# A decoder block on one core: Strassen's seven block products in half of the feed-forward's second product

## The chip, the cores and the metric

One core of one Trainium2 chip runs the whole kernel. The metric is the device time of one execution in microseconds, the median of several runs.

## The reference

A decoder block for 256 tokens of width 2048: gated short convolution and sparse attention side by side, a layer norm, then a feed-forward of width 8192, a gated per-layer embedding and a second layer norm. The change lies in the last part:

```python
x = _layer_norm(DN_ALPHA * x + mixed @ w_mix_out[i], ln1_g[i], ln1_b[i])

h = jnp.square(jax.nn.relu(x @ w_mlp_up[i])) @ w_mlp_down[i]
ple = (p[i] @ w_ple[i]) * jax.nn.sigmoid(x @ w_ple_gate[i])
x = _layer_norm(DN_ALPHA * x + h + ple, ln2_g[i], ln2_b[i])
```

`x` is 256 x 2048, `w_mlp_up` 2048 x 8192 and `w_mlp_down` 8192 x 2048, all float32.

## The kernel before

**Precision.** Each float32 operand is split in two float32r parts, a high part (ACT copies it, rounding) and a low part (DVE subtracts the high part from the original). A product is three matmuls: high x high, low x high, high x low.

**Weights.** `wchunk` (line 83) loads 512 KB of a weight matrix by SP's queue into `raw` (four buffers), and makes `whi` on ACT (line 91, four buffers) and `wlo` on DVE (line 93, three buffers). Each of the 648 chunks of the kernel goes this way.

**Two forms of product.** `wstat` (line 96) keeps weights stationary: a block of 256 columns of weights against all 256 tokens, 16 k-tiles in four chunks. For each k-tile it issues two matmuls of 512 columns (line 110: high weights against both parts of the tokens) and two of 256 (line 117: low weights against the high tokens). `xstat` (line 127) keeps tokens stationary: a block of 512 weight columns moves past them, 16 k-tiles in eight chunks, and for each k-tile six matmuls of 512 (lines 139, 140, 143), three for each 128 tokens.

**The feed-forward** (line 750 on) has four chunks of 2048 hidden columns. In each, the up stage is eight `wstat` blocks ("pairs" below, since each gives two tiles of 128 hidden columns). After each, `ev_up` adds the two parts in PSUM, applies relu and square, and splits the result into `h`. Then the down stage is four `xstat` blocks over `h` (`down`, line 775), added into `y`. In the fourth chunk the last block has its weights loaded ahead (`last_weights`, line 791).

**Order.** The program is written in sequence; a scheduling layer then orders the instructions of each engine and sets the semaphores. `issue_after` holds an instruction behind a named one. Each engine and each DMA queue takes its instructions in that order.

**Other names.** The gate stage (lines 714 to 728) multiplies `ple` by a sigmoid, and loads `gb` (g and b of the first layer norm, broadcast) through POOL's queue. `residual` (line 687) forms g, b and the residual sum in `y`, one 512-column piece after each of the first eight up blocks. PSUM has eight banks: four for `mm`, two `sc`, one `tp`, one `po`.

Of the kernel before, what the change touches and what calls it, by code (L numbers as in the profile page):

```python
# [10 lines left out]
F32 = mybir.dt.float32  # L11
F32R = mybir.dt.float32r
# [33 lines left out]
def block_kernel(ctx: ExitStack, tc: tile.TileContext, x, p, w_in, conv_w, cmp_pe_k, cmp_w1_k, cmp_w2_k,  # L46
# [12 lines left out]
    ps_mm = ctx.enter_context(tc.tile_pool(name="ps_mm", bufs=4, space=bass.MemoryType.PSUM))  # L59
    ps_sc = ctx.enter_context(tc.tile_pool(name="ps_sc", bufs=2, space=bass.MemoryType.PSUM))  # L60
    ps_tp = ctx.enter_context(tc.tile_pool(name="ps_tp", bufs=1, space=bass.MemoryType.PSUM))
    ps_po = ctx.enter_context(tc.tile_pool(name="ps_po", bufs=1, space=bass.MemoryType.PSUM))
# [14 lines left out]
    def load_raw(src, nk, n):  # L77

        raw = wp.tile([P, nk, n], F32, tag="raw", name="raw", bufs=4)
        nc.sync.dma_start(raw, src.rearrange("(k p) n -> p k n", p=P))  # L80
        return raw

    def wchunk(src, nk, n, behind=None):


        raw = load_raw(src, nk, n)
# [9 lines left out]
    def wstat(src, c0, mov, evac, r0=0, nk=4, ahead=None, behind=None):  # L96


        ps = [ps_mm.tile([P, 2, T], F32, tag="mm", name="mm") for _ in range(2)]
        for k0 in range(0, KT, nk):  # L100
            hi, lo = wchunk(src[r0 + k0 * P:r0 + (k0 + nk) * P, c0:c0 + 256], nk, 256,
                            behind(k0 // nk) if behind is not None else None)
            for kk in range(nk):
                kt = k0 + kk
                if ahead is not None:
                    ahead(kt)

                def high():
                    for f in range(2):
                        last_mm[0] = nc.tensor.matmul(  # L110
                            ps[f].rearrange("p a t -> p (a t)"), hi[:, kk, f * P:(f + 1) * P],
                            mov[:, kt].rearrange("p a t -> p (a t)"), start=(kt == 0), stop=(kt == KT - 1),
                            skip_group_check=True).ins

                def low():
                    for f in range(2):
                        last_mm[0] = nc.tensor.matmul(ps[f][:, 1, :], lo[:, kk, f * P:(f + 1) * P],  # L117
                                                      mov[:, kt, 0, :], start=False, stop=False,
                                                      skip_group_check=True).ins
# [4 lines left out]
        for f in range(2):  # L124
            evac(f, ps[f][:, 0, :], ps[f][:, 1, :])

    def xstat(src, c0, n, sta, evac, r0=0, nkt=KT, ahead=None, behind=None):

        ps = [ps_mm.tile([P, n], F32, tag="mm", name="mm") for _ in range(NT)]
        for k2 in range(nkt // 2):  # L130
            hi, lo = wchunk(src[r0 + k2 * 256:r0 + (k2 + 1) * 256, c0:c0 + n], 2, n,
# [100 lines left out]
    with tc.tile_pool(name="front", bufs=1) as fp:  # L232
# [79 lines left out]
        def compress(i, w1, w2):  # L312
# [3 lines left out]
            for l4 in range(CMP_LEN // 4):  # L316
                hi, lo = wchunk(w1[0][l4 * 512:(l4 + 1) * 512, :], 4, HID)
# [357 lines left out]
    x1_lo, gated = [], []  # L675
# [11 lines left out]
    def residual(t, j):  # L687

        cs = slice(j * 512, (j + 1) * 512)
        v = y[:, t, cs]  # L690
        nc.vector.tensor_mul(v, v, gb[:, 0, cs])
        nc.vector.tensor_add(v, v, gb[:, 1, cs])
        nc.vector.scalar_tensor_tensor(v, v, ALPHA, ple[:, t, cs], op0=ALU.mult, op1=ALU.add)
# [20 lines left out]
    for j in range(4):  # L714
        cs = slice(j * 512, (j + 1) * 512)

        def ev_gate(t, ps):
            sg = post.tile([P, 512], F32, tag="sg", name="sg")
            nc.scalar.activation(sg, ps, AF.Sigmoid)
            gated.append(nc.vector.tensor_mul(ple[:, t, cs], sg, ple[:, t, cs]).ins)  # L720

        run(xstat(w_ple_gate, j * 512, 512, x1, ev_gate, ahead=x1_ahead if j == 0 else None,
                  behind=(lambda k2: x1_lo[k2 - 1] if k2 else normed) if j == 0 else None))
        if j in (1, 3):

            with after(gated[2 * j - 1]):
                nc.vector.memset(gb[:, j // 2, 0:1], 0.0)
            nc.gpsimd.dma_start(gb[:, j // 2, :], (ln1_g, ln1_b)[j // 2].to_broadcast([P, D]))


    stats2 = post.tile([P, NT, 4, 6], F32, tag="st", name="stats2", bufs=1)
    gb2 = big.tile([P, 2, D], F32, tag="O", name="gb2")
# [17 lines left out]
    done_up = []  # L750
    for c in range(4):
        if c % 2 == 0:
            h = big.tile([P, KT, 2, T], F32R, tag="B", name="h")
        else:
            h = post.tile([P, KT, 2, T], F32R, tag="C", name="h", bufs=1)
        for f2 in range(0, KT, 2):

            def ev_up(f, a, b):
                m = post.tile([P, T], F32, tag="m", name="m", bufs=3)
                nc.scalar.activation(m, a, AF.Copy)  # L760
                nc.vector.tensor_add(m, m, b)
                nc.vector.scalar_tensor_tensor(m, m, 0.0, m, op0=ALU.max, op1=ALU.mult)
# [102 lines left out]
```

## Time and profile before

| | us |
|---|---|
| median of 3 runs (1834.59 to 1834.60) | 1834.59 |
| the profiled execution | 1835.34 |
| its span, first to last instruction | 1833.3 |
| PE busy | 1818.7 |
| DVE busy | 1132.0 |
| ACT busy | 867.7 |
| one up stage (eight `wstat` blocks) | 89.32 |
| one down stage (four `xstat` blocks) | 87.05 |

PE is TensorE's matmuls, DVE VectorE, ACT ScalarE, POOL GpSimd, SP the engine that issues most DMAs. A matmul's record ends by a model, so the pace of a stream of matmuls is read from start to start: the length of a stage over the number of its matmuls.

### The profile page before, as it was taken

The numbers are of one execution on the slowest core, as the hardware profiler recorded it, in microseconds if no ns is written. First come the engines' busy times: TensorE is split into PE (matmuls) and PEld (weight loads), VectorE is DVE, ScalarE is ACT, GpSimd is POOL, SyncE is SP. The second block draws the span as 40 slices with busy tenths as digits, with TensorE's granted clock in tenths as the row PEclk, the third lists the DMA queues.
The fourth block names the chain that finished last, engine by engine and source line by source line (L and its number), as shares of the span: only waits on it lengthen the run. The fifth ranks groups of instructions, "written<-read, shape, count | busy, mean of one in ns | idle before, by whom it ended". The sixth has DMA issues, their size and how long they took to land.

```text
span 1833.3 us, 24899 instructions
## 1 busy us (share of the span) xinstructions
PE 1818.7 (99%) x9412; PEld 1552.1 (85%) x9412; DVE 1132.0 (62%) x1657; ACT 867.7 (47%) x1207; POOL 24.7 (1%) x37
## 2 busy tenths in 40 slices
PE   9999999999999999999999999999999999999997
PEld 7889888888888888888888888888888888888886
DVE  6776777777787444455555656765665556556664
ACT  5555555455555444444443744543444345434550
POOL 1000000000000000000000000000000000000001
PEclk9999999999999999999999999999999999999999
DMA  8777665555656666666655567655665666566671
GB/s 249 229 244 213 176 174 171 172 164 170 173 162 198 221 195 193 191 191 188 192 185 195 176 221 234 190 191 194 193 187 194 191 208 217 189 195 190 196 246 46
DMA packets 261272, 352.92 MB, mean 193 GB/s; under 512 B 11125, under 2 KB 175317, under 8 KB 260384
## 3 DMA queue, kind: packets, MB, share of 16 engines
q1 hardware_dynamic: 256384, 338.08, 60.1%
q0 software_dynamic: 2112, 8.81, 1.5%
q10 hardware_dynamic: 2656, 4.46, 0.7%
q8 instruction: 73, 1.20, 0.3%
q14 instruction: 47, 0.39, 0.1%
HBM read 349.17 MB, written 2.12 MB: 192 GB/s over the span
## 4 chain that ended last, share of the span: by engine, by line
PE 60%; issue 37%; DMA 1%; DVE 0%; POOL 0%; ACT 0%; POOLq 0%; SPq 0%
PE mm L110 16%; PE mm L143 10%; PE mm L140 10%; PE mm L139 10%; PE mm L117 8%; PE mm L807 1%; DMA rawl<-in_w_mlp_down_dram 1%; PE pss L471 1%; PE ph L321 1%; PE tp L194 1%; PE po L543 1%; PE tp L534 1%; PE po L550 0%; DMA xnat<-in_x_dram 0%; ACT wh L71 0%
## 5 line engine op out<-in xcount | busy, mean ns | idle before, releaser
L93 DVE TENSOR_TENSOR wlo<-raw,whi 128x1024 fp32r<-128x1024 f32 (+2 forms) x648 | 780.1, 1205 | 595.7 <-PE mm L143 337.9
L91 ACT ACTIVATE whi<-raw 128x1024 fp32r<-128x1024 f32 (+2 forms) x648 | 677.4, 1047 | 728.0 <-PE mm L140 444.1
L110 PE MATMUL mm<-xT,whi 128*128 128x512 f32 x1280 | 405.5, 399 | 0.1
L110 PE MATMUL mm<-x,whi 128*128 128x512 f32 x1024 | 316.8, 395 | 0.0
L117 PEld LDWEIGHTS mm<-xT,wlo 128*128 128x128 f32 x1280 | 233.8, 189 | 50.9 <-DVE wlo L93 0.2
L117 PE MATMUL mm<-xT,wlo 128*128 128x256 f32 x1280 | 249.0, 280 | 0.0
L117 PEld LDWEIGHTS mm<-x,wlo 128*128 128x128 f32 x1024 | 187.9, 188 | 42.5
L110 PEld LDWEIGHTS mm<-xT,whi 128*128 128x128 f32 x1280 | 199.4, 190 | 3.7 <-ACT whi L91 1.2
L117 PE MATMUL mm<-x,wlo 128*128 128x256 f32 x1024 | 196.7, 279 | 0.0
L140 PE MATMUL mm<-whi,h 128*128 128x512 f32 x480 | 186.7, 389 | 0.0
L139 PE MATMUL mm<-whi,h 128*128 128x512 f32 x480 | 186.7, 389 | 0.0
L110 PEld LDWEIGHTS mm<-x,whi 128*128 128x128 f32 x1024 | 158.4, 189 | 2.8
L143 PE MATMUL mm<-wlo,h 128*128 128x512 f32 x480 | 147.9, 389 | 0.4 <-DVE wlo L93 0.4
L139 PE MATMUL mm<-whi,xT 128*128 128x512 f32 (+1 forms) x352 | 130.1, 373 | 0.0
L140 PE MATMUL mm<-whi,xT 128*128 128x512 f32 (+1 forms) x352 | 130.0, 373 | 0.0
L143 PEld LDWEIGHTS mm<-wlo,h 128*128 128x128 f32 x480 | 90.0, 188 | 19.4 <-DVE wlo L93 0.8
L140 PEld LDWEIGHTS mm<-whi,h 128*128 128x128 f32 x480 | 90.1, 188 | 18.8
L139 PEld LDWEIGHTS mm<-whi,h 128*128 128x128 f32 x480 | 90.1, 188 | 18.7
L143 PE MATMUL mm<-wlo,xT 128*128 128x512 f32 (+1 forms) x352 | 102.7, 373 | 0.0
L139 PEld LDWEIGHTS mm<-whi,xT 128*128 128x128 f32 x352 | 66.1, 188 | 11.2
L140 PEld LDWEIGHTS mm<-whi,xT 128*128 128x128 f32 x352 | 66.1, 188 | 11.2
L143 PEld LDWEIGHTS mm<-wlo,xT 128*128 128x128 f32 x352 | 63.4, 188 | 10.5
(226 smaller groups left out, 1776.3 us busy)
## 6 DMA issues: line engine op xcount, KB each, us to landing
raw<-in_w_in_dram SPq DMA_DIRECT2D x228, 512.0 KB, 3.7
raw<-in_w_mlp_up_dram SPq DMA_DIRECT2D x128, 512.0 KB, 3.9
raw<-in_w_mlp_down_dram SPq DMA_DIRECT2D x120, 512.0 KB, 4.0
raw<-in_w_conv_out_dram SPq DMA_DIRECT2D x32, 512.0 KB, 3.7
raw<-in_w_attn_out_dram SPq DMA_DIRECT2D x32, 512.0 KB, 3.6
raw<-in_w_mix_out_dram SPq DMA_DIRECT2D x32, 512.0 KB, 3.7
raw<-in_w_ple_gate_dram SPq DMA_DIRECT2D x32, 512.0 KB, 3.9
raw<-in_w_in_dram SPq DMA_DIRECT2D x16, 280.0 KB, 3.2
```

The lines of the kernel that those rows point to most:

```text
L91: nc.scalar.activation(hi, raw, AF.Copy)
L93: last_wlo[0] = nc.vector.tensor_sub(lo, raw, f32(hi)).ins
L110: last_mm[0] = nc.tensor.matmul(ps[f].rearrange("p a t -> p (a t)"), hi[:, kk, f * P:(f + 1) * P], mov[:, kt].rearrange("p a t -> p (a t)" ...
L117: last_mm[0] = nc.tensor.matmul(ps[f][:, 1, :], lo[:, kk, f * P:(f + 1) * P], mov[:, kt, 0, :], start=False, stop=False, skip_group_check= ...
L139: nc.tensor.matmul(ps[t], sta[:, kt, 0, ts], hi[:, kk, :], start=(kt == 0), stop=False)
L140: nc.tensor.matmul(ps[t], sta[:, kt, 1, ts], hi[:, kk, :], start=False, stop=False)
L143: last_mm[0] = nc.tensor.matmul(ps[t], sta[:, kt, 0, ts], lo[:, kk, :], start=False, stop=(kt == nkt - 1)).ins
L194: nc.tensor.transpose(tp[:, k, t * P:(t + 1) * P], nat[:, t, (kt + k) * P:(kt + k + 1) * P], ident)
L321: nc.tensor.matmul(ph, blk[:, i, l].rearrange("p a n -> p (a n)"), part[:, k, :], start=(part is hi and l == 0), stop=(part is lo and l == ...
L471: nc.tensor.matmul(ps, q[:, g, a, t * P:(t + 1) * P], kT[:, j, c, c0:c0 + n], start=(i == 0), stop=(i == 2))
L534: nc.tensor.transpose(tp[:, b, k, :], s[:, b, 1 - k if t and b == 0 else k], ident)
L543: nc.tensor.matmul(po, vn[:, b, 0, a, vs], pT[:, c, b, 0:2], start=(n == 0 and b == 0), stop=False, skip_group_check=True)
```

## The change

**Seven products.** In chunks 0 to 2, `down` computes only the columns 1024 to 2047 as before. For columns 0 to 1023, each pair p of k-tiles is a product of 2 x 2 blocks: the tokens in two halves of 128, the hidden columns in two tiles of 128, the weight columns in two halves of 512. Seven block products (Strassen's, in the form with few sums) take the place of eight. Six are accumulated over p in six PSUM banks (`products`, 18 matmuls for each p). The seventh, plain one comes last, as 24 matmuls from weights that are loaded a second time.

**What feeds them.** `up` makes four sums of blocks of h on DVE (`sa`) and splits them (`sums`). `load` fetches the 1 MB of weights of a pair as one transfer; `b_forms` splits the two plain blocks, `t_sums` makes four sums of blocks on DVE, and `t_forms` splits those. After the last product ten DVE operations and one ACT copy combine the six banks into `y`.

**Where.** `products(p - 2)` and the preparation of pair p - 1 are written between the chunks of pair p; the scheduling layer moves them further.

**`ev_up`** becomes: ACT copies both PSUM banks, DVE adds, ACT applies Relu and Square, then the split, 512 columns at a time.

**Order in `wstat`, everywhere in the kernel.** All 512-column matmuls of a chunk come together, then its 256-column ones, and in every other chunk (and the last) the other way round. In the feed-forward (`ps` given) the matmuls of one PSUM bank also come together.

**The rest.** `residual` is taken apart by operation and woven into the gate stage, with the loads of `gb` ahead of it. PSUM is divided anew before the feed-forward. `h` has one buffer in place of two; `wl` and the later `gb2` move. Nothing else changes.

```diff
-            for kk in range(nk):
-                kt = k0 + kk
...
-                for part in ((high, low) if kt < KT - 1 else (low, high)):
-                    part()
+            last = k0 + nk == KT
+            parts_ = (low, high) if last or ahead is None and k0 // nk % 2 == 1 else (high, low)
+            if apart:
+                order = [(part, kk, f) for part in parts_ for f in range(2) for kk in range(nk)]
+                if last:
+                    order.sort(key=lambda o: o[2])
+            else:
+                order = [(part, kk, f) for part in parts_ for kk in range(nk) for f in range(2)]
+            for part, kk, f in order:
+                part(kk, f)
             yield
...
+    def up(c, p, banks):
+
+        ps = [b.rearrange("p (a t) -> p a t", a=2) for b in banks]
+        yield from wstat(w_mlp_up, c * 2048 + p * 256, x1, None, ps=ps)
+        ab = post.tile([P, 2, 2, T], F32, tag="m2", name="ab", bufs=2)
+        for f in range(2):
+            nc.scalar.activation(ab[:, f], ps[f], AF.Copy)
+        m = ab[:, :, 0, :]
+        nc.vector.tensor_add(m, m, ab[:, :, 1, :])
+        nc.scalar.activation(m, m, AF.Relu)
+        nc.scalar.activation(m, m, AF.Square)
+        split(m, h[:, 2 * p:2 * p + 2, 0, :], h[:, 2 * p:2 * p + 2, 1, :])
         if c < 3:
-            run(*(down(j)[0] for j in range(4)))
+
+            sa = post.tile([P, 4, P], F32, tag="pn", name="sa", bufs=1)
+            b11, b12, b21, b22 = (m[:, k, t * P:(t + 1) * P] for t in range(2) for k in range(2))
+            nc.vector.tensor_add(sa[:, 0, :], b21, b22)
+            nc.vector.tensor_sub(sa[:, 1, :], sa[:, 0, :], b11)
+            nc.vector.tensor_sub(sa[:, 2, :], b11, b21)
+            nc.vector.tensor_sub(sa[:, 3, :], b12, sa[:, 1, :])
+            sums[p] = post.tile([P, 4, 2, P], F32R, tag="sg", name="sums")
+            split(sa, sums[p][:, :, 0, :], sums[p][:, :, 1, :])
...
+        def load(p):
+            if p % 2 == 0:
+                raws[p] = post.tile([P, 2, 1024], F32, tag="rs", name="rs", bufs=1)
+            else:
+                raws[p] = tr[:, 4:8].rearrange("p (k a) n -> p k (a n)", k=2)
+            nc.sync.dma_start(raws[p], rows[:, p, :, 0:1024])
+
+        def b_forms(p):
+            r = raws[p]
+            b = forms[:, 8 + p % 2 * 4:12 + p % 2 * 4]
+            split(back(r, 0, (1536, 2), (1, 512)), b[:, 0:2], b[:, 2:4])
+
+        def t_sums(p):
+            r = raws[p]
+            nc.vector.tensor_sub(tf[:, 0:2], r[:, :, 512:], r[:, 0, :].rearrange("p (a n) -> p a n", a=2))
+            nc.vector.tensor_sub(tf[:, 2], r[:, 1, 512:], tf[:, 0])
+            nc.vector.tensor_sub(tf[:, 3], tf[:, 2], r[:, 1, :512])
+
+        def t_forms(p):
+            for i in (0, 2):
+                split(tf[:, i:i + 2], forms[:, i:i + 2], forms[:, 4 + i:6 + i])
+
+        def products(p, which):
...
+                for i, (a, w) in enumerate(((0, hi), (1, hi), (0, lo))):
+                    last_mm[0] = nc.tensor.matmul(acc[n], first[:, a, :], forms[:, w, :], start=(p == 0 and i == 0),
+                                                  stop=(p == 7 and i == 2)).ins
+
+        prep = (b_forms, t_sums, t_forms)
+        for p in range(8):
+            pair = up(c, p, [bank(6), bank(7)] if p == 1 else [bank(0), bank(1)])
+            for i in range(4):
+                if p >= 2 and i in (0, 2):
+                    products(p - 2, (5, 7, 6, 4) if i else (1, 3))
+                next(pair)
+                if i == 2:
+                    load(p)
+                if p >= 1 and i < 3:
+                    prep[i](p - 1)
+            run(pair)
+        products(6, (1, 3, 5, 7, 6, 4))
+        third = down(c, 2, [bank(0), bank(1)])[0]
+        for i in range(8):
+            next(third)
...
+        run(down(c, 3, [bank(2), bank(3)])[0])
+        ps = bank(4)
+        for q in range(0, 8, 2):
+            hi, lo = wchunk(rows[:, q:q + 2, 1, 0:512], 2, 512)
...
```

**The order on PE, third pair of the second chunk.** Before, in every up block, with `mm` the PSUM banks, `x_9126` the tokens:

```order
L117 MATMUL mm<-x_9126,wlo 128x256 x2
L110 MATMUL mm<-x_9126,whi 128x512 x2
L117 MATMUL mm<-x_9126,wlo 128x256 x2
L110 MATMUL mm<-x_9126,whi 128x512 x2
L117 MATMUL mm<-x_9126,wlo 128x256 x2
```

In the changed kernel, from the end of that pair through the fourth (`u` and `s` are PSUM banks, L860 the block products; those of the second pair stand here):

```order
L116 MATMUL u<-x_9126,wlo 128x256 x4
L110 MATMUL u<-x_9126,whi 128x512 x4
L860 MATMUL s<-forms,h 128x512 x3
L860 MATMUL s<-forms,sums 128x512 x12
L860 MATMUL s<-forms,h 128x512
L110 MATMUL u<-x_9126,whi 128x512 x4
L116 MATMUL u<-x_9126,wlo 128x256 x2
L110 MATMUL u<-x_9126,whi 128x512 x4
L116 MATMUL u<-x_9126,wlo 128x256 x14
L110 MATMUL u<-x_9126,whi 128x512 x8
L860 MATMUL s<-forms,h 128x512 x2
L110 MATMUL u<-x_9126,whi 128x512 x8
```

The sizes, which took turns by two, stand in runs, and 16 of the 18 block products have moved to the front of the pair.

**The order on DVE at the same place.** Before, one up block:

```order
L93 TENSOR_TENSOR wlo<-raw,whi 128x1024 x3
L761 TENSOR_TENSOR m<-m,mm 128x256 x2
L762 SCALAR_TENSOR_TENSOR m<-m 128x256 x2
L72 TENSOR_TENSOR h<-m,h 128x256
L93 TENSOR_TENSOR wlo<-raw,whi 128x1024
L72 TENSOR_TENSOR h<-m,h 128x256
```

In the changed kernel, from the add that ends the third pair (L792) to just before the next one; the first `wlo` here is that of the fourth pair's last chunk:

```order
L792 TENSOR_TENSOR ab<-ab 128x2x256
L73 TENSOR_TENSOR forms<-tr,forms 128x1024 x2
L800 TENSOR_TENSOR sa<-ab 128x128
L802 TENSOR_TENSOR sa<-ab 128x128
L843 TENSOR_TENSOR tr<-tr 128x1024
L801 TENSOR_TENSOR sa<-sa,ab 128x128
L73 TENSOR_TENSOR h<-ab,h 128x2x256
L92 TENSOR_TENSOR wlo<-raw,whi 128x1024
L803 TENSOR_TENSOR sa<-ab,sa 128x128
L92 TENSOR_TENSOR wlo<-raw,whi 128x1024
L73 TENSOR_TENSOR sums<-sa,sums 128x4x128
L73 TENSOR_TENSOR forms<-tr,forms 128x1024
```

Two low parts of forms and the sums now stand between the add and the low part of the next weight chunk.

**The order on SP at the end of the second chunk.** Before, the down stage and the next up stage are two rows:

```order
L80 DMA raw<-in_w_mlp_down_dram 128x2x512 x32
L80 DMA raw<-in_w_mlp_up_dram 128x4x256 x32
```

In the changed kernel (`rs` and `tr` receive the 1 MB loads, line 834; the last four `raw` of the down weights are the seventh product's):

```order
L834 DMA rs<-in_w_mlp_down_dram 128x2x1024
L85 DMA raw<-in_w_mlp_down_dram 128x2x512 x9
L834 DMA tr<-in_w_mlp_down_dram 128x2x1024
L85 DMA raw<-in_w_mlp_down_dram 128x2x512 x4
L834 DMA rs<-in_w_mlp_down_dram 128x2x1024
L85 DMA raw<-in_w_mlp_down_dram 128x2x512 x4
L834 DMA tr<-in_w_mlp_down_dram 128x2x1024
L85 DMA raw<-in_w_mlp_up_dram 128x4x256 x19
```

The next chunk's first four 1 MB loads have moved among the loads of this chunk's last blocks.

## Rows read from the trace of the kernel before

**Rows 1.** The page, part 1: busy us (share of the span) xinstructions

```profile
PE 1818.7 (99%) x9412; PEld 1552.1 (85%) x9412; DVE 1132.0 (62%) x1657; ACT 867.7 (47%) x1207; POOL 24.7 (1%) x37
```

**Rows 2.** Waits of PE, whole span: us in total, times, longest us

```profile
PE pw L258 <- DVE tab L272: 1.5, 1, 1.5
PE tp L194 <- DMA xnat<-in_x_dram: 1.0, 2, 0.5
PE mm L143 <- DVE wlo L93: 0.4, 1, 0.4
```

**Rows 3.** Stages: down, up, down, up (chunks 0 to 2)

```profile
core 0: us, PE busy (x) PEld busy (x) DVE busy (x) ACT busy (x) POOL busy (x), PEclk, DMA share, GB/s
1204.73:1291.78 87.05, 87.05 (x385) 72.10 (x384) 46.50 (x48) 35.49 (x37) 0.00 (x0) 1.00 0.60 193
1291.78:1381.10 89.32, 89.32 (x513) 77.98 (x512) 55.17 (x77) 42.78 (x61) 0.00 (x0) 1.00 0.64 189
1381.10:1468.15 87.05, 87.05 (x385) 72.07 (x384) 44.69 (x45) 35.49 (x37) 0.00 (x0) 1.00 0.60 193
```

**Rows 4.** Waits in the up stage 1291.78 to 1381.10

```profile
ACT whi L91 <- PE mm L110: 27.8, 16, 1.9
DVE wlo L93 <- PE mm L117: 21.8, 16, 1.6
```

**Rows 5.** PE in order of time, a run of 256s; start us, us recorded

```profile
61.43 0.63 PE L321 MATMUL ph<-whi,blk 128*120 128x256 f32 x4
61.90 0.63 PE L321 MATMUL ph<-wlo,blk 128*120 128x256 f32 x4
62.36 0.62 PE L110 MATMUL mm<-xT,whi 128*128 128x512 f32 x2
```

**Rows 6.** PE in order of time, where one up block meets the next

```profile
1301.99 0.64 PE L117 MATMUL mm<-x,wlo 128*128 128x256 f32 x4
1302.46 1.09 PE L110 MATMUL mm<-x,whi 128*128 128x512 f32 x4
1303.39 0.40 PE L117 MATMUL mm<-x,wlo 128*128 128x256 f32 x2
```

**Rows 7.** Groups of instructions by form: xcount | busy us, mean ns

```profile
L93 DVE TENSOR_TENSOR wlo<-raw,whi 128x1024 fp32r<-128x1024 f32 x223 | 272.8, 1224 | 225.4 <-PE mm L143 111.2 <-PE mm L117 70.5 <-issue 38.9
L72 DVE TENSOR_TENSOR x<-m,x 128x512 fp32r<-128x512 f32 x8 | 5.5, 689 | 4.4 <-ACT x L71 4.3
L343 DVE TENSOR_TENSOR g<-g,g 128x120 f32<-128x120 f32 x2 | 0.6, 283 | 0.1
L71 ACT ACTIVATE wh<-rawl 128x1024 fp32r<-128x1024 f32 x8 | 8.5, 1062 | 11.4 <-DMA rawl<-in_w_mlp_down_dram 11.4
L602 ACT ACTIVATE sg<-mm 128x512 f32<-128x512 f32 x16 | 8.6, 585 | 4.2 <-PE mm L143 4.2
L71 ACT ACTIVATE x<-m 128x512 fp32r<-128x512 f32 x8 | 5.0, 630 | 0.1
L745 ACT ACTIVATE y<-y,nm,r 128x512 f32<-128x512 f32 x2 | 1.6, 816 | 34.8 <-DVE nm L737 34.8
```

**Rows 8.** DVE in order of time, dependent operations and one that is not

```profile
1198.04 0.69 DVE L691 TENSOR_TENSOR y<-y,ple_gb 128x512 f32<-128x512 f32 x1
1198.76 0.69 DVE L692 TENSOR_TENSOR y<-y,ple_gb 128x512 f32<-128x512 f32 x1
1199.40 1.23 DVE L93 TENSOR_TENSOR wlo<-raw,whi 128x1024 fp32r<-128x1024 f32 x1
1200.55 0.69 DVE L693 SCALAR_TENSOR_TENSOR y<-y,ple_gb 128x512 f32<-128x512 f32 x1
```

**Rows 9.** The ten microseconds with the most traffic

```profile
590.00:600.00 10.00, 10.00 (x46) 8.29 (x45) 3.81 (x4) 5.33 (x6) 0.00 (x0) 1.00 0.99 382
```

**Rows 10.** The last two of the four gate blocks

```profile
1071.90:1115.42 43.52, 43.52 (x194) 36.04 (x192) 22.02 (x21) 18.94 (x21) 0.54 (x1) 1.00 0.67 218
```

More of the change, by code (lines that the diff above doesn't have):

```diff
@@ L102, in wstat @@
                             behind(k0 // nk) if behind is not None else None)
-            for kk in range(nk):
-                kt = k0 + kk
[L105 to L119, printed above, removed]
-                for part in ((high, low) if kt < KT - 1 else (low, high)):
-                    part()
+            if ahead is not None:
+                for kk in range(nk):
+                    ahead(k0 + kk)
@@ L123, in wstat, with xstat @@
             yield
-        for f in range(2):
+        for f in range(2 if evac is not None else 0):
             evac(f, ps[f][:, 0, :], ps[f][:, 1, :])
-    def xstat(src, c0, n, sta, evac, r0=0, nkt=KT, ahead=None, behind=None):
-        ps = [ps_mm.tile([P, n], F32, tag="mm", name="mm") for _ in range(NT)]
+    def xstat(src, c0, n, sta, evac, r0=0, nkt=KT, ahead=None, behind=None, ps=None):
+        if ps is None:
+            ps = [ps_mm.tile([P, n], F32, tag="mm", name="mm") for _ in range(NT)]
@@ L685, in x1_turn, with residual, gb_load, steps_of @@
         x1_lo.append(split(m, x1[:, kt0:kt0 + 2, 0, :], x1[:, kt0:kt0 + 2, 1, :]))
-    def residual(t, j):
+    def residual(i, j):
         cs = slice(j * 512, (j + 1) * 512)
[L690 to L693, printed above, removed]
+        for t in range(NT):
+            v = y[:, t, cs]
+            with after(last_wlo[0]):
+                if i == 2:
+                    nc.vector.scalar_tensor_tensor(v, v, ALPHA, ple[:, t, cs], op0=ALU.mult, op1=ALU.add)
+                else:
+                    nc.vector.tensor_tensor(v, v, gb[:, i, cs], op=(ALU.mult, ALU.add)[i])
+    def gb_load(dst, i, v):
+        with after(last_wlo[0]):
+            nc.vector.memset(dst[:, i, 0:1], 0.0)
+        nc.gpsimd.dma_start(dst[:, i, :], v.to_broadcast([P, D]))
+    def steps_of(*calls):
+        for f, *args in calls:
+            f(*args)
+            yield
     normed = x1_norm(0)
@@ L719, in ev_gate, with bank @@
             nc.scalar.activation(sg, ps, AF.Sigmoid)
[L720 to L728, printed above, removed]
+            nc.vector.tensor_mul(ple[:, t, cs], sg, ple[:, t, cs])
+        places, side = (((), ()),
+                        ((0, 4), ((gb_load, gb, 0, ln1_g), (gb_load, gb, 1, ln1_b))),
+                        ((1, 2, 3, 4, 5, 6), [(residual, 0, i) for i in range(4)] + [(residual, 1, 0), (residual, 1, 1)]),
+                        ((1, 2, 3, 4, 6), ((residual, 1, 2), (residual, 1, 3), (residual, 2, 0), (residual, 2, 1),
+                                           (residual, 2, 2))))[j]
+        weave(xstat(w_ple_gate, j * 512, 512, x1, ev_gate, ahead=x1_ahead if j == 0 else None,
+                    behind=(lambda k2: x1_lo[k2 - 1] if k2 else normed) if j == 0 else None),
+              places, steps_of(*side))
+    residual(2, 3)
+    psum.close()
+    ps_s = ctx.enter_context(tc.tile_pool(name="ps_s", bufs=1, space=bass.MemoryType.PSUM))
+    ps_u = ctx.enter_context(tc.tile_pool(name="ps_u", bufs=2, space=bass.MemoryType.PSUM))
     stats2 = post.tile([P, NT, 4, 6], F32, tag="st", name="stats2", bufs=1)
-    gb2 = big.tile([P, 2, D], F32, tag="O", name="gb2")
+    def bank(i):
+        if i < 2:
+            return ps_u.tile([P, 512], F32, tag="u", name="u")
+        return ps_s.tile([P, 512], F32, tag=f"s{i - 2}", name="s")
     def finish(t, mine=1536):
```

134 lines of the change are left out of this document (84 added, 50 removed).

## The prediction, made before the changed kernel ran

> **What bounds the kernel now.** First the page's busy shares: PE has work for 99% of the span, DVE for 62%, ACT for 47% [rows 1]. A busy PE alone says little, so second comes the list of what PE waited for: three entries, 2.9 us in 1833, one of them, 0.4 us, for a low part from DVE [rows 2]. Third, the stages of the feed-forward: an "up" stage takes 89.32 us and a "down" stage 87.05 us, PE fills both, and in an up stage DVE works 55 us and ACT 43 us of 89 [rows 3]. In that stage ACT and DVE wait for PE, 16 times each, 1.7 and 1.4 us a time, and not the other way [rows 4]. So the span is PE's matmul stream; a change is worth the matmul time that it removes, as long as DVE, ACT and the weight transfers still come before PE.
>
> **The rates.** A down stage is 384 matmuls of 512 columns (4 column blocks x 16 k-tiles x 6): 87.05/384 = 226.7 ns each. An up stage is 8 blocks of 32 matmuls of 512 columns and 32 of 256. At 226.7 ns the 512s are 58.04 us of the 89.32, which leaves 31.28/256 = 122.2 ns for a 256 in the present order, two 512s and two 256s in turn. The granted clock is 1.00 in these stages (its upper level, 2.4 GHz).
>
> **Part 1, fewer matmuls.** In three chunks the half of the down product with columns 0 to 1023 had 192 matmuls of 512. Seven block products instead of eight make 168: 144 woven into the up stage and 24 behind the last column block. 3 x 24 = 72 matmuls go, 72 x 226.7 ns = **16.3 us**. All of this is on PE, so all of it is on the path.
>
> **Part 2, the order inside a column block.** Everywhere that weights are the stationary side, PE now takes the 512s of a chunk together and then its 256s, and every other chunk the other way round. In the built order the size changes 394 times in place of 2084 over the 72 blocks (2304 matmuls of each size). What a longer run is worth is not in the trace as such. Best case: eight 256s in a row took 0.93 us, 116.3 ns each [rows 5], with the 512s at 226.7; then 5.9 ns per pair of sizes, for the 81% of changes that go: 2304 x 5.9 x 0.81 = 11.0 us. Worst case: where one block meets the next there are four 256s in 0.47 us and four 512s in 0.93 us, 350.0 ns for the two against 348.9 in turn [rows 6]: a loss of 2304 x 1.1 ns = 2.5 us. The new runs are 8 to 16 long, nearer to the down stage and to the run of eight than to runs of four; I take a gain of **6 us**.
> What the Trainium skill says bears on both parts: its page "TensorE: Matmul & The Clock Gate", section "Back-to-back issue gap", gives N/2.4 + 2.5 ns for a matmul at full clock, 215.8 ns for 512 columns and 109.2 for 256, with no word of a mix. By that rule part 1 is 72 x 215.8 = 15.5 us and part 2 nothing. The rows above are slower by 11 and 13 ns, so the rule misses something that order may change, and the rows decide.
>
> **Part 3, what DVE and ACT get.** From row durations [rows 7], for one of the eight column-block pairs of an up stage with its products: DVE has 4 low parts x 1.22, the add and the low part of h 2 x 0.69, four sums of 128 columns x 0.29 (nearest row: 120 columns at 0.28), their low part 0.69, one low part of the plain weight blocks 1.22, the weight sums 1.22 + 2 x 0.69, and two low parts of these 2 x 1.22: 14.4 us. PE has 11.17 + 18 x 0.2267 = 15.25 us. ACT has 4 x 1.06 + 2 x 0.585 + 4 x 0.63 + 3 x 1.06 = 11.1 us (Relu and Square, not in the trace, are taken as the copy of 512, 0.63; Identity with scale at 0.82 would add 0.4). So DVE is at 94% by plain sums. DVE operations that don't need each other overlap: the one at 1200.55 starts 0.08 before the end of the one at 1199.40, while a dependent one at 1198.76 starts 0.03 after its source [rows 8]. Between the two DVE's pair costs 13.1 to 14.9 us. Work fits, without room to spare.
> Against this stands the Trainium skill, page "VectorE: DVE Perf Modes", section "The DRAIN you can't avoid": the next operation does not start until the pipe has emptied. By that rule the lower of the two DVE figures falls away and DVE stands at 94% or more; the row at 1200.55 speaks for overlap where nothing is shared.
> Whether it also comes in time is a matter of order. In the order shown for the third pair, from PE's end of a pair (t = 0): PE does 16 products (3.63), two weight chunks (5.58), 2 products (0.45), a third chunk (2.79), and at 12.45 needs the low part of the fourth chunk. DVE must first have the PSUM copies (about 0.8), the add (to 1.5), and two low parts of forms, whose buffers come free after 6 and after 12 products (1.36, 2.72), each behind ACT's copy (1.06): the second is done at 2.72 + 1.06 + 1.22 = 5.0. Then two sums 0.57, a weight sum 1.22, a sum 0.29, the low part of h 0.69 and the low part that PE needs 1.22: **9.0 against 12.45**, 3.4 us ahead. The PSUM banks that the next pair writes are free after about 0.8 and 1.5, and PE wants them at 3.63. So I cost this part at nothing; if the 3.4 us go, every microsecond behind them counts 18 times (six pairs in three chunks).
>
> **Part 4, the seams.** Near the end of a chunk DVE has ten combining operations of 512 (10 x 0.69 = 6.9 us) among the low parts of the third column block, then PE runs through four weight transfers in 24 matmuls, 5.4 us, less time per transfer than anywhere before. The lower bound is nothing; the upper is all ten in front of a low part that PE needs, 6.9 us x 3. DVE's buffers of three low parts and the eight chunks of the fourth column block absorb most of it. I take **2 us** for the three seams, with 10 us for the range.
>
> **Part 5, transfers.** A chunk moved 64 loads of 0.52 MB, 33.6 MB; now 2.1 MB are read again for the seventh product, 35.7 MB in about 171 us (89.32 + 360 x 0.2267), 209 GB/s against 193 and 189 now [rows 3]. In the seam it is more: three loads of 1 MB and twelve of 0.5 MB in about 28 us, 330 GB/s. The trace has 382 GB/s over 10 us with the queues 99% busy [rows 9]. It fits, and its shortfall is in the seam's range above. On SP's queue the big loads stand among the weight loads; each waits for a DVE step that the next weight load nearly waits for too.
>
> **Part 6, the rest.** The 24 residual operations (0.69 each, 16.6 us of DVE) leave the first up stage for the last two gate blocks, where DVE works 22 us of 43.5 [rows 10]; the two broadcast loads of g and b on POOL's queue, each behind a DVE memset of one column, both start in the second gate block now, and nothing but these operations waits for them: nothing for PE. The end (last matmul to last store) has the same operations: nothing.
>
> **The sum.** The profiled execution took 1835.34 us, 2.0 over its span of 1833.3, and 0.75 more than the median of the runs, 1834.59. 1835.34 - 16.3 - 6 + 2 = 1815.0, and 0.75 less for the runs: **1814.3 us**. Ends: 16.3 + 11.0 and no seam loss give 1807.3; 16.3, a loss of 2.5 in the order and 10 at the seams give 1830.8, an unlikely pair, so I stop at 1827.
>
> **Rivals.**
> A, the order is worth nothing: the 512s stay at 232 ns in a stage that has 256s too, in any order. For it: the run of four [rows 6]. Against: the steady 226.7 of the down stage. 1814.3 + 6 = 1820.3 us. (The Trainium skill's section named in part 2 would have it so.)
> B, slower: DVE and ACT in lockstep with PE. Each form is written only after the products that read its buffer, first by ACT and then by DVE, and all low parts stand behind it in DVE's one queue. If DVE can't use its waits, a pair costs 14.4 of work, 0.8 for the copies and 2.4 (1.36 + 1.06) until the first form: 17.6 against 15.25, 2.4 us x 18 = 42 us, so 1856 us. It turns slower than before when each of the 18 pairs loses more than (22.3 - 2)/18 = 1.1 us. Against: the 3.4 us of lead, and that the waits lie beside one another.
> C, the seams cost their upper bound, 20.7 us in place of 2: 1833.0, no change that can be told.
>
> **Chances.** Forecast 0.65, A 0.22, B 0.07, C 0.06. A measurement here tells 0.2% (3.7 us) from no change. Faster 0.87, same 0.06, slower 0.07. Eight in ten are held by 1806 to 1827: forecast, A, and the lower part of the seam costs.
>
> **What would show it.** PE's count falls by 72. Part 1: block products at 227 ns each. Part 2: a block of 64 in the early stages (before the feed-forward) takes 11.08 us instead of 11.17; at 11.17 A is right, and under 11.05 the best case. Part 3: PE's list of waits stays at a few us; B shows as waits of PE for the low part of a fourth chunk or for a form, every pair. Part 4: waits of PE just behind the combining operations or at the four late transfers. The forecast is wrong above all if PE's waits for DVE in the three up stages add up to more than 10 us.

## The result, and the profile of the changed kernel

The changed kernel takes 1817.95 us, the median of five runs (1817.47 to 1820.43), against 1834.59: the ratio is 0.9912, 95% interval 0.9901 to 0.9923. That is 16.6 us less, where 20.3 were forecast. The profiled execution took 1817.73 us with a span of 1815.9; the prediction's own sum for it was 1815.0.

The page's first part, to be laid beside [rows 1] (busy us, share of the span, instructions):

```profile
PE 1801.0 (99%) x9340; PEld 1544.0 (85%) x9340; DVE 1236.2 (68%) x1778; ACT 959.9 (53%) x1302; POOL 24.7 (1%) x37
```

PE has 72 matmuls less and is still busy for 99% of the span. DVE has 104 us more work and ACT 92 us, and PE hardly waits longer for them than before. The list of PE's waits over the whole span (us in total, times, longest), which answers to [rows 2]:

```profile
PE pw L267 <- DVE tab L281: 1.5, 1, 1.5
PE tp L203 <- DMA xnat<-in_x_dram: 0.7, 1, 0.7
PE mm L116 <- DVE wlo L92: 0.6, 1, 0.6
PE mm L148 <- ACT whi L90: 0.3, 1, 0.3
PE u L110 <- ACT whi L90: 0.2, 1, 0.2
```

Only the last of them lies in the three chunks with block products. The 0.6 us (at 22 us) and the 0.3 us (at 114) lie in the early stages and come with the new order: all nine traces of kernels with that order have both, and the two with the old order, here and below, have 0.1 us at the first place and nothing at the second. So the kernel is bound as before, by PE's stream, and the question is what this stream costs now. Two stretches, the whole second chunk (up, products and what is left of the down stage) and the up stage of the fourth, where no products are; they answer to [rows 3]:

```profile
core 0: us, PE busy (x) PEld busy (x) DVE busy (x) ACT busy (x) POOL busy (x), PEclk, DMA share, GB/s
1287.95:1458.89 170.94, 170.94 (x874) 146.06 (x872) 138.79 (x171) 105.13 (x126) 0.00 (x0) 1.00 0.64 209
1629.79:1717.27 87.48, 87.48 (x505) 77.14 (x504) 48.98 (x51) 53.22 (x69) 1.09 (x2) 1.00 0.69 222
```

The second chunk took 89.32 + 87.05 = 176.37 us and takes 170.94: 5.43 less, and 24 matmuls of 226.7 ns are 5.44. The products and the new order together gave what was forecast for the products alone; the kernel with the old order, below, tells the two apart. The second line has 504 of the 512 matmuls of its up stage, since 8 of 512 columns were drawn ahead into the end of the third chunk; with 8 x 0.2267 it is 89.29 us, against 89.32. The new order gave next to nothing there. PE in order of time at the start of that stage (start us, us recorded; a run's real length is the distance to the next start):

```profile
1629.79 2.08 PE L116 MATMUL u<-x,wlo 128*128 128x256 f32 x16
1631.70 3.82 PE L110 MATMUL u<-x,whi 128*128 128x512 f32 x16
1635.36 1.11 PE L116 MATMUL u<-x,wlo 128*128 128x256 f32 x8
1636.31 0.40 PE L110 MATMUL s<-x,whi 128*128 128x512 f32 x1
1636.54 0.65 PE L116 MATMUL u<-x,wlo 128*128 128x256 f32 x4
1637.02 1.09 PE L110 MATMUL u<-x,whi 128*128 128x512 f32 x4
1637.95 0.64 PE L116 MATMUL u<-x,wlo 128*128 128x256 f32 x4
1638.42 1.09 PE L110 MATMUL u<-x,whi 128*128 128x512 f32 x4
```

Sixteen 256s take 1.91 us (119 ns each), sixteen 512s 3.66 (228.8 ns). A run of four 512s takes 0.93 (232.5 ns), as in [rows 6]. The runs are there; what they save is small, and at a block's end runs of four are left.

### The profile page after: what moved, and what is told of

Its sections match the earlier page's. It is cut to its first block, busy times and chain, and to the rows that moved or that the text cites. A ratio compares the mean times of both kernels' runs of the same rounds, so it can differ in the third digit from the quotient of the medians.

```text
span 1815.9 us, 24871 instructions
## 1 busy us (share of the span) xinstructions
PE 1801.0 (99%) x9340; PEld 1544.0 (85%) x9340; DVE 1236.2 (68%) x1778; ACT 959.9 (53%) x1302; POOL 24.7 (1%) x37
## 4 chain that ended last, share of the span: by engine, by line
PE 97%; DMA 1%; DVE 1%; ACT 0%; issue 0%; POOLq 0%; POOL 0%; SPq 0%; ACTq 0%; DVEq 0%
PE mm L110 16%; PE mm L148 10%; PE mm L149 10%; PE mm L152 10%; PE u L110 9%; PE mm L116 8%; PE s L860 5%; PE u L116 5%; PE s L110 4%; PE s L116 2%; PE s L148 2%; PE s L149 2%; PE s L152 2%; PE u L149 2%; PE u L152 2%; PE u L148 2%
## 5 line engine op out<-in xcount | busy, mean ns | idle before, releaser
L110 PE MATMUL mm<-xT,whi 128*128 128x512 f32 x1280 | 313.5, 393 | 0.0
L110 PE MATMUL u<-x,whi 128*128 128x512 f32 x736 | 190.4, 392 | 0.2 <-ACT whi L90 0.2
L116 PE MATMUL mm<-xT,wlo 128*128 128x256 f32 x1280 | 181.6, 285 | 0.6 <-DVE wlo L92 0.6
L116 PEld LDWEIGHTS mm<-xT,wlo 128*128 128x128 f32 x1280 | 170.0, 190 | 8.2 <-DVE wlo L92 0.8
L110 PEld LDWEIGHTS u<-x,whi 128*128 128x128 f32 x736 | 132.4, 188 | 24.1 <-ACT whi L90 0.8
L116 PEld LDWEIGHTS u<-x,wlo 128*128 128x128 f32 x736 | 100.9, 190 | 7.6
L116 PE MATMUL u<-x,wlo 128*128 128x256 f32 x736 | 103.1, 282 | 0.0
L73 DVE TENSOR_TENSOR forms<-tr,forms 128x1024 fp32r<-128x1024 f32 x60 | 72.3, 1220 | 25.0 <-ACT forms L72 24.9
L860 PE MATMUL s<-forms,sums 128*128 128x512 f32 x288 | 73.2, 389 | 0.0
L110 PE MATMUL s<-x,whi 128*128 128x512 f32 x288 | 71.9, 392 | 0.0
L72 ACT ACTIVATE forms<-tr 128x1024 fp32r<-128x1024 f32 x60 | 62.2, 1050 | 10.4 <-PE s L860 6.7
L860 PEld LDWEIGHTS s<-forms,sums 128*128 128x128 f32 x288 | 54.0, 188 | 11.4
```

Of the source, the lines that this page charges most:

```text
L72: last_hi[0] = nc.scalar.activation(hi, src, AF.Copy).ins
L73: last_lo[0] = nc.vector.tensor_sub(lo, src, f32(hi)).ins
L110: last_mm[0] = nc.tensor.matmul(ps[f].rearrange("p a t -> p (a t)"), hi[:, kk, f * P:(f + 1) * P], mov[:, k0 + kk].rearrange("p a t -> p ( ...
L860: last_mm[0] = nc.tensor.matmul(acc[n], first[:, a, :], forms[:, w, :], start=(p == 0 and i == 0), stop=(p == 7 and i == 2)).ins
```

## The experiments

**What a run of one size is worth.** Four kernels are the kernel before with another order in its column blocks and nothing else. With `order` in place of the loop over k-tiles (`high` and `low` are the matmuls of 512 and 256 columns):

```
 r1:  order = [(part, kk, f) for kk in range(nk) for f in range(2) for part in (high, low)]
 r4:  order = [(part, kk, f) for k1 in range(0, nk, 2) for part in (high, low)
               for kk in range(k1, k1 + 2) for f in range(2)]
 r8:  order = [(part, kk, f) for part in (high, low) for kk in range(nk) for f in range(2)]
 r16: the same, with (low, high) in every other chunk
```

In each, the low part comes first at the very end of a block, as in the kernel before. This turn joins two runs, so half of the matmuls of r8 stand in runs of 16, and a quarter of those of r4 in runs of 8.

> The kernel before with the changed order in its column blocks and nothing else: all 512s of a chunk, then its 256s, every other chunk the other way round, so runs of 16. Up stage of the second chunk 89.32 us before. Prediction (a longer run is worth 2.6 ns per pair of sizes): the up stage 88.65 us, the kernel 6 us faster, 1828.6. Theory 1 (each change of size costs 3.0 ns, (89.32 - 256 x 0.3461)/240, whatever the run ahead; 32 changes per stage left): 88.70 us, kernel 1829 to 1830. Theory 2 (what one cycle of sizes costs grows with the run; a cycle of 16 and 16 took 3.654 + 1.913 us in the changed kernel): 16 x 5.567 = 89.07 us, kernel 1832 to 1833. Rival A: 89.32 and 1834.6.

> The kernel before with runs of 8 (all 512s of a chunk, then its 256s, the same way in each chunk; 48 changes of size per up stage in place of 240). Up stage of the second chunk, 89.32 before: theory 1 (fixed price per change) 88.74 us; theory 2 (price per cycle grows with the run) 89.1 to 89.4 us; rival A 89.32.

> The kernel before with runs of 4 (two k-tiles' 512s, then their 256s; 112 changes of size per up stage in place of 240). Up stage of the second chunk, 89.32 before: theory 1 (fixed price per change) 88.93 us; theory 2 (a cycle of 4 and 4 took 0.93 + 0.47 us) 89.4 to 89.6 us, slower than runs of 2; rival A 89.32.

> The kernel before with runs of 1 (a 512 and a 256 in turn; 496 changes of size per up stage in place of 240). Up stage of the second chunk, 89.32 before: theory 1 (fixed price per change) 90.1 us; theory 2 sets no value for it beyond less than 89.4 us if the price of a cycle falls with the run; rival A 89.32.

The up stage of the second chunk, with the columns as above, for runs of 1:

```profile
1293.87:1384.27 90.40, 90.40 (x514) 78.44 (x513) 54.37 (x77) 42.83 (x61) 0.00 (x0) 1.00 0.62 187
```

of 4:

```profile
1293.07:1382.77 89.70, 89.70 (x513) 78.53 (x513) 55.71 (x77) 42.84 (x61) 0.00 (x0) 1.00 0.62 188
```

of 8:

```profile
1291.57:1380.80 89.23, 89.23 (x514) 78.69 (x513) 56.15 (x77) 41.55 (x61) 0.00 (x0) 1.00 0.61 189
```

and of 16:

```profile
1290.25:1379.32 89.07, 89.07 (x514) 78.71 (x513) 55.53 (x77) 41.54 (x61) 0.00 (x0) 1.00 0.60 189
```

With the 89.32 of runs of 2 [rows 3] the series is 90.40, 89.32, 89.70, 89.23, 89.07 us for 1, 2, 4, 8 and 16. The third and fourth up stages of the same five traces repeat these lengths to 0.01 us, so the differences are not scatter. Theory 1, one price for each change of size, falls: by it runs of 4 would have taken 88.93, and they are slower than runs of 2. Theory 2 gave 89.07 for runs of 16 from two rows of the changed kernel, and that is what came; runs of 4 are 0.1 us above its range. Runs of 1 fit neither: theory 1 gave 90.1 for them, theory 2 less than 89.4. A run of 16 saves 0.25 us per up stage, not the 0.67 us (6 us x 8 of 72 blocks) that the prediction took. As a whole kernel, runs of 16 measured 1833.51 against 1834.44 (ratio 0.9992, 0.9983 to 1.0001): 0.9 us, not told from nothing. The other three ran once each, in 1842.56 (r1), 1837.43 (r4) and 1836.49 us (r8). That r8 is slower than the kernel before although its stages are shorter has another place: in its trace PE loses 2.6 us at the last weights, 0.6 in the kernel before.

**The products without the order.** The changed kernel with the old order:

```diff
-            last = k0 + nk == KT
-            parts_ = (low, high) if last or ahead is None and k0 // nk % 2 == 1 else (high, low)
...
+            order = [(part, kk, f) for kk in range(nk)
+                     for part in ((high, low) if k0 + kk < KT - 1 else (low, high)) for f in range(2)]
```

> The changed kernel with the old order in its column blocks (two 512s and two 256s in turn), so Strassen's products alone. Prediction: the order is worth 6 us, so 1824. Theory 2 (an up stage of runs of 16 took 89.07 us, one of runs of 2 89.32, over 9 such stages in all): 1818.5 to 1820, and the three chunks of the feed-forward 16 us shorter than before by the products alone. Rival A: 1818.

1819.99 us against 1834.34 for the kernel before, ratio 0.9922 (0.9909 to 0.9934): the products alone are worth 14.4 us net of their seams, where 1.1 us of PE's time is lost in this trace. The order is worth about 2.0 us on top of them (1819.99 against the 1817.95 above); as the intervals of the two ratios overlap, this is not clear of the scatter. Between the two traces 0.8 us of it lies before the feed-forward and 0.6 is a larger seam loss. It is not 6. The third chunk, where this trace shows no seam loss:

```profile
1459.32:1630.40 171.08, 171.08 (x873) 145.60 (x872) 132.29 (x162) 100.08 (x121) 1.46 (x2) 1.00 0.60 191
```

It is 5.29 us below the 176.37 of a chunk before. So the products alone, without a seam loss, gave 5.3 us per chunk with the old order, 15.9 in three, and not the whole 16.3. The difference may lie in the built order, where the products break the old order's runs of 2 into 134 single 256s and some 110 single 512s, and single ones are dear by the series above; this was not tried apart.

**Where the order went in the feed-forward.** The changed kernel without its regrouping in the last chunk of a block:

```diff
-                if last:
-                    order.sort(key=lambda o: o[2])
```

> The changed kernel without the regrouping by PSUM bank in a block's last chunk, which left two runs of 4 and 4 in each block of the feed-forward; its runs are now 8 to 16 there. Theory 2 (runs of 4 are dear, 89.70 us for a stage of them, 89.07 for runs of 16): the fourth chunk's up stage loses its runs of 4 and its 504 matmuls, 87.48 us, take 87.1 to 87.3; over the four chunks 0.6 to 1.2 us, 1817. If both PSUM banks now ending together makes PE wait (the first bank's copy starts 0.5 us later): waits of PE for the banks in every pair, 0.3 to 0.8 us each, 6 to 14 us slower, 1824 to 1832. Rival A (no order is worth anything): 1818.

The fourth chunk's up stage, the same 504 matmuls:

```profile
1630.17:1717.43 87.26, 87.26 (x505) 77.20 (x504) 48.98 (x51) 53.24 (x69) 1.10 (x2) 1.00 0.68 223
```

87.26 in place of 87.48, as theory 2 had it: the runs of 4 that this regrouping leaves had eaten the gain of the longer ones. All 512 matmuls of the stage, counted from the first to the next stage's first, take 89.07 us here and 89.29 to 89.31 in all seven traces with the regrouping. No wait of PE for a PSUM bank came up. The whole kernel took 1817.83 us (0.9906, 0.9890 to 0.9923), not told from the 1817.95; its seams lost 0.6 us more in this trace than they lost above.

**How much room DVE has.** The sum of 1024 columns is computed two or three times over, with the same result, as load on DVE alone:

```diff
+            for _ in range(2):        # three in the second kernel
                 nc.vector.tensor_sub(tf[:, 0:2], r[:, :, 512:], ...)
```

> The changed kernel with the weight sum of 1024 columns computed twice for each pair, one more DVE operation of 1.22 us in each of 24 pairs. Theory L (DVE's operations overlap: it was busy 13.25 of 15.25 us per pair, so 14.4 now): no more than 1 us slower, 1818 to 1819. Theory S (plain sums: 14.4 + 1.22 = 15.6 over 15.25): 0.37 us in 18 to 24 pairs, 7 to 9 us slower, 1825 to 1827. Rival B (already in lockstep): 1.2 us in each of 18 pairs, 22 us.

> The same with that sum computed three times, two more DVE operations per pair. Theory L: 13.25 + 2 x 1.14 = 15.53 over 15.25, 0.28 us in 18 to 24 pairs, 5 to 7 us slower, 1823 to 1825, with PE now waiting for low parts. Theory S: 16.84 over 15.25, 1.6 us a pair, 29 to 38 us slower, 1847 to 1856. Rival B: 44 us.

One more operation cost nothing: 1818.1 us (0.9912, 0.9897 to 0.9927). Two more cost 6 us: 1824.08 (0.9946, 0.9932 to 0.9960). Both numbers are theory L's, but its place for the second, a loss in each pair, is wrong; that the second number fits is luck. The third to the eighth pair of the second chunk, summed over six windows, in the changed kernel, with one, and with two more operations:

```profile
sum 91.46, PE 91.46 PEld 79.17 DVE 78.02 ACT 62.61 POOL 0.00; mean PE 15.24 PEld 13.20 DVE 13.00 ACT 10.43 POOL 0.00
```

```profile
sum 91.74, PE 91.74 PEld 79.41 DVE 82.44 ACT 62.58 POOL 0.00; mean PE 15.29 PEld 13.23 DVE 13.74 ACT 10.43 POOL 0.00
```

```profile
sum 91.56, PE 91.56 PEld 79.19 DVE 85.39 ACT 61.19 POOL 0.00; mean PE 15.26 PEld 13.20 DVE 14.23 ACT 10.20 POOL 0.00
```

A pair keeps its 15.25 us even with two more operations: DVE rises to 14.23 us a pair, and part of the work moves out to the chunk's ends. There it costs. DVE in order of time at the first seam, with two more operations:

```profile
1285.91 3.48 DVE L92 TENSOR_TENSOR wlo<-raw,whi 128x1024 fp32r<-128x1024 f32 x3
1289.32 1.21 DVE L844 TENSOR_TENSOR tr<-tr 128x1024 f32<-128x1024 f32 x1
1290.45 1.21 DVE L73 TENSOR_TENSOR forms<-tr,forms 128x1024 fp32r<-128x1024 f32 x1
1291.59 1.21 DVE L92 TENSOR_TENSOR wlo<-raw,whi 128x1024 fp32r<-128x1024 f32 x1
```

and PE there (with its idle time and the releaser behind):

```profile
1289.58 1.11 PE L116 MATMUL u<-x,wlo 128*128 128x256 f32 x8
1292.86 1.22 PE L116 MATMUL u<-x,wlo 128*128 128x256 f32 x8 [2.16 <-DVE wlo L92]
```

An added sum (L844) and a low part of a form stand ahead of the low part that PE needs, which ends at 1292.80; PE starts at 1292.86. By the starts, PE's losses behind the start of the feed-forward add up to 5.4 us in this kernel, all at the first two seams, most of them for low parts. So with this load the narrow place is where one chunk meets the next, not the pair.

**What the seams cost, and why.** In the changed kernel PE loses 0.5 us at the first seam (two matmuls, 0.38 and 0.11 us longer than their kind) and nothing that shows at the other two. PE, then ACT in order of time, there:

```profile
1284.24 0.61 PE L903 MATMUL s<-whi,h 128*128 128x512 f32 x2
1285.08 2.11 PE L110 MATMUL u<-x,whi 128*128 128x512 f32 x8 [0.22 <-ACT whi L90]
```

```profile
1283.97 1.06 ACT L90 ACTIVATE whi<-raw 128x1024 fp32r<-128x1024 f32 x1 [2.54 <-DMA raw<-in_w_mlp_up_dram]
```

PE waits for ACT's high part, and ACT has waited 2.5 us for the transfer of the next chunk's first weights. Eight microseconds earlier ACT had stood longer still, for a weight chunk of the seventh product that SP issued 1.1 us behind a 1 MB load:

```profile
1275.90 1.06 ACT L90 ACTIVATE whi<-raw 128x1024 fp32r<-128x1024 f32 x1 [5.73 <-DMA raw<-in_w_mlp_down_dram]
```

Four edits change what is transferred there and when. In the first, each 1 MB load is held on SP's queue behind the up weights of its own pair:

```diff
-            nc.sync.dma_start(raws[p], rows[:, p, :, 0:1024])
+            with after(last_raw[0]):      # the latest load of a weight chunk
+                nc.sync.dma_start(raws[p], rows[:, p, :, 0:1024])
```

> The changed kernel with each 1 MB load held on SP's queue behind the up weights of its own pair, so that none of them stands among the seam's loads any more (4 MB less there). If the seam's 0.5 us of PE waits (18 matmuls at 248 ns and 8 at 244 in the first seam) come from transfers that are late: these go, 1817.0 to 1817.5. If the forms of the first pairs then come late: PE waits in the second and third pair of each chunk, 1 to 3 us in each, up to 1827.

It is not faster than the changed kernel but some 3 us slower: 1820.93 us (0.9924, 0.9912 to 0.9937). The intervals of the two ratios overlap, but its trace shows the loss: 1.9 us at the first seam and 1.3 at the second. ACT behind the first seam:

```profile
1285.49 1.06 ACT L90 ACTIVATE whi<-raw 128x1024 fp32r<-128x1024 f32 x1 [2.75 <-DMA raw<-in_w_mlp_up_dram]
1289.30 1.06 ACT L72 ACTIVATE forms<-rs 128x1024 fp32r<-128x1024 f32 x1 [2.75 <-DMA rs<-in_w_mlp_down_dram]
1291.52 1.06 ACT L90 ACTIVATE whi<-raw 128x1024 fp32r<-128x1024 f32 x1 [1.15 <-DMA raw<-in_w_mlp_up_dram]
1292.48 1.04 ACT L72 ACTIVATE forms<-tr 128x1024 fp32r<-128x1024 f32 x1
1293.43 2.13 ACT L90 ACTIVATE whi<-raw 128x1024 fp32r<-128x1024 f32 x2
```

and PE:

```profile
1291.80 1.11 PE L116 MATMUL u<-x,wlo 128*128 128x256 f32 x8
1294.52 2.12 PE L110 MATMUL s<-x,whi 128*128 128x512 f32 x8 [1.61 <-ACT whi L90]
```

ACT takes its instructions in order. It stood 2.75 us before a form whose load, issued at 1281.8, was not yet there, and the high parts of the next weights, which PE needs first, stood behind it, after a further 1.15 us for a chunk of up weights and one more form. Here loads that are early but unused cost less in the seam than loads that are late and in front of something.

In the second, only the loads of the third and later pairs are held so; in the third, the seventh product's four weight chunks are woven into the last column block; the fourth has both:

```diff
-        run(down(c, 3, [bank(2), bank(3)])[0])
-        ps = bank(4)
-        for q in range(0, 8, 2):
+        fourth = down(c, 3, [bank(2), bank(3)])[0]
+        ps = bank(4)
+        for j in range(8):
+            next(fourth)
+            if j % 2 == 0:
+                continue
+            q = j - 1
             hi, lo = wchunk(rows[:, q:q + 2, 1, 0:512], 2, 512)
```

> The changed kernel with only the 1 MB loads of the third and later pairs held behind their own pair's up weights, so two of the four 1 MB loads leave the seam and the first two stay. If the volume in the seam is what makes its transfers late: the waits of 0.5 us go, 1817.0 to 1817.6. If what counts is that ACT finds a form's load done when its turn comes (in the run with all loads held, ACT stood 2.8 us before one, and the next high part of weights behind it): the first two loads are as early as before, and the third now stands nearer to its use: 1818 to 1820.

> The changed kernel with the seventh product's four weight chunks woven into the last column block (one after every second chunk) in place of all behind it, so that its four transfers no longer follow one another in 24 matmuls (5.4 us). If the seam's waits come from that burst: no PE wait between the end of the last block and the next chunk's second pair, 0.5 us off the trace of the changed kernel, and runs of 1817.0 to 1817.6. If the burst has no part in it: 1818. If DVE's combining now meets the woven low parts: PE waits in the last block, 1 us a seam, 1821.

> Both edits together. If burst and volume each have a part: 1817.0 to 1817.5 and no PE wait at the seams. If neither has: 1818.

The second took 1818.12 us (0.9907, 0.9890 to 0.9923), with no loss at the seams in its trace: all three of its chunks take 170.9 us, where the first of the changed kernel took 171.4. The third took 1820.23 (0.9920, 0.9905 to 0.9935), the fourth 1817.91 (0.9906, 0.9891 to 0.9921). The woven kernel only moved the loss into the last block, as PE there in the second chunk shows:

```profile
1448.20 0.73 PE L907 MATMUL s<-whi,h 128*128 128x512 f32 x2 [0.98 <-ACT whi L90]
```

with, in the same block of the first chunk, ACT waiting for transfers (us in total, times, longest):

```profile
ACT whi L90 <- DMA raw<-in_w_mlp_down_dram: 7.4, 7, 5.1
```

The fourth kernel did the same: its trace has no loss between the chunks, but PE loses 1.3 us in the last block of the first one, behind ACT's high part. So in the trace of the changed kernel the seam's loss is transfers that come late, and none of the four beats that kernel beyond the measurement. The size of the loss in one execution, 0.5 us in three seams, is less than the scatter between executions, and no edit showed that it can be had back.

## Why the prediction was right, and where it was off

The direction, the bound and the range held; the time came out 3.7 us above the forecast. That it missed by no more is in part luck: the order fell some 5 us short, and the seams and the last weights gave 2 us of that back. Point by point:

- **Part 1, fewer matmuls: right.** 16.3 us were forecast; the second chunk gave 5.43 with the new order, three times that 16.3, and 15.9 is what the old order shows. The block products come at 227 ns, as the prediction asked: in the rows of part 3, twelve of them take 2.73 us from start to start, 227.5 ns each. The 15.5 us that the prediction sets beside it is an estimate from the 215.8 ns of the Trainium skill, "TensorE: Matmul & The Clock Gate", section "Back-to-back issue gap". The section calls that formula the gap of an isolated matmul and gives about 131 ns for 512 columns in a sustained stream, which the prediction left out; the chunk's 5.43 us over 24 are 226 ns, so the measurement agrees with neither.
- **Part 2, the order: the step that failed, by its size.** I took 6 us between a gain of 11.0 and a loss of 2.5. The stage of runs of 16 gained 0.25 us, over nine such stages 2.2 us, and the changed kernel, whose feed-forward has runs of 4 too, got only a part of that. Between its two forms the kernel showed 0.9 (order alone) and 2.0 us (order on top of the products), neither of them clear of the scatter. The best case put two prices together, 116.3 ns for a 256 in a run [rows 5] and 226.7 for a 512, and took both from elsewhere than a column block. The matmuls of [rows 5] are of another form, 128*120 with 120 stationary columns, where the blocks' are 128*128. By the starts in the up stages, a 256 of the kernel before took 116.0 ns already and a 512 232.9, not 122.2 and 226.7 as the prediction divided them; in runs of 16 they take 119.5 and 228.4. Deep in a run they come at 120 and 226.7, so even runs without an end would save 2.2 ns per pair of sizes, an estimated 5 us in 2304 pairs and less than the 6 forecast. The two waits that the order brings in the early stages, 0.9 us, had no term either. Only [rows 6] had a whole cycle of both sizes, and it said loss; I should have given it more weight than a run of one size. The sign I gave was right for runs of 16, and a block of the early stages fell by less than the 0.09 us forecast: the first long stretch of them, 144 such matmuls, in the changed kernel and in the kernel before:

```profile
167.99:193.14 25.15, 25.15 (x147) 22.21 (x146) 17.40 (x28) 14.78 (x24) 0.00 (x0) 1.00 0.71 214
```

```profile
167.71:192.88 25.17, 25.17 (x147) 22.00 (x146) 17.56 (x28) 14.23 (x23) 0.00 (x0) 1.00 0.71 203
```

- **Part 3, DVE and ACT: right, with its working.** A pair was to take 15.25 us of PE and takes 15.24, DVE 13.1 to 14.9 and takes 13.0, at the end of full overlap, ACT 11.1 and takes 10.4. At the place that the prediction worked out (here the products that start at 1323.68), the low part of the fourth chunk was to be there 9.0 us later. DVE:

```profile
1326.40 2.36 DVE L73 TENSOR_TENSOR forms<-tr,forms 128x1024 fp32r<-128x1024 f32 x2 [0.42 <-ACT forms L72]
1329.13 1.22 DVE L843 TENSOR_TENSOR tr<-tr 128x1024 f32<-128x1024 f32 x1
1331.07 1.22 DVE L92 TENSOR_TENSOR wlo<-raw,whi 128x1024 fp32r<-128x1024 f32 x1
1332.21 0.28 DVE L803 TENSOR_TENSOR sa<-ab,sa 128x128 f32<-128x128 f32 x1
```

and PE:

```profile
1323.68 0.85 PE L860 MATMUL s<-forms,h 128*128 128x512 f32 x3
1324.37 2.89 PE L860 MATMUL s<-forms,sums 128*128 128x512 f32 x12
1327.10 0.39 PE L860 MATMUL s<-forms,h 128*128 128x512 f32 x1
1335.17 1.60 PE L116 MATMUL u<-x,wlo 128*128 128x256 f32 x12
```

  The forms' low parts end at 1328.76, 5.1 us after the start (5.0 forecast), the low part at 1332.29, 8.6 us after it (9.0). PE needs it after eight of the twelve 256s, at 1336.1, 12.4 us after (12.45). The lead is 3.8 us. One added DVE operation was free, so DVE had room; rival B, lockstep, falls. The row at 1332.21 starts 0.08 us before the one ahead of it ends. At plain sums one more operation would have cost 7 to 9 us; it cost 0.2 us, which is within the scatter. The prediction cited for plain sums the Trainium skill, "VectorE: DVE Perf Modes", section "The DRAIN you can't avoid", but left out a sentence of the same section, "A next op that is not held starts earlier". The trace's 0.08 us agrees with that sentence.
- **Part 4, the seams: right in kind, too dear.** 2 us were taken, 0.5 measured in this execution (1.1 in the traces of two of the other orders). The cause was not the ten combining operations, which the prediction put first: PE waited for no low part there. It was the second half of that part, the transfers. Rival C falls.
- **Part 5, transfers: right in sum.** 209 GB/s were forecast and 209 came in the second chunk. In the seam they do not fit without loss in every execution.
- **Part 6: right.** PE's list has no wait for the gate stage or the residual.
- **Outside the sum.** PE's wait at the last weights [rows 2], a matmul there that was 0.5 us late in the kernel before, did not come in this execution. It is back in four of the eight other traces of kernels with the products (0.3 to 0.9 us), and all five traces of kernels without them have it (0.6 to 2.6 us). So it varies by itself, and how much of the 0.6 us gained there is the change's stays open.

The sum, made again with what was measured: 16.3 in the three chunks by the products and the order, 0.7 gained before the feed-forward (its first matmul at 1114.72 in place of 1115.42; other traces with the new order have 1113.5 to 1115.1), 0.5 lost at the seams, 0.6 not lost at the last weights, 0.2 less outside the span: 17.3 us of the 17.6 between the two profiled executions. Rival A, an order that is worth nothing, came nearest in its mechanism: its 1820.3 less the 1.5 us that the seams cost too much there is 1818.8, 0.9 above the result. It had 0.22; the forecast's 0.65 was too much for a price that no row showed as such.

## What to carry to other kernels

Where one engine's stream is the whole time, count its instructions and multiply by the pace of the stage: that part held to 0.5 us in 16. A price for their order must be read from a whole cycle of the mix, both sizes and in the same form of matmul, and not from a run of one of them; if there is no such row, the nearest mix decides and not the purer run. Here the work woven onto a second engine was first late where the stages meet, not in the steady loop, and a load that is held back to ease a busy stretch can cost more than it frees when an in-order engine has to wait for it ahead of other work.

## What the hardware did that was not expected

The same 512 matmuls of an up stage, 256 of each size, took 90.40, 89.32, 89.70, 89.23 and 89.07 us in runs of 1, 2, 4, 8 and 16. Runs of 4 are slower than runs of 2, which no price per change of size gives; within a run the first 256s come quickest (four in 0.47 us, 118 ns each; sixteen in 1.91, 119) and the first 512s behind them slowest (232.5 ns in a run of four between 256s, 228.8 in one of sixteen). Matmul by matmul, from start to start in the kernel with runs of 16, the 256s of a run take 113, 119 and then 120 ns each, and the 512s behind them 233, 236, 228, 233, 231 and from the sixth on 226.7. So a change from 256 to 512 costs 27 ns there, spread over five 512s, of which a run of four pays 22; a 256 in a short run saves a few of these. That gives the order of the series: beyond 346.7 ns for a pair of sizes, runs of 1 pay 6 ns, runs of 2 pay 2, runs of 4 nearly 4, runs of 16 a little over 1. Why the first five are slow stays open. The spread between the orders that a kernel would use, 2 to 16, is 0.7% of the stage, and the granted clock was 1.00 in all of them.
